# Issuing a decoder kernel's weight loads from ScalarE's DMA queue, with new costs in its planner

## The chip, the cores and the metric

The kernel runs on one core of a Trainium2 chip. The metric is the time of one execution in device microseconds, as the median of three runs. Only this core works; there is no exchange with others.

## The reference, cut to what matters

One step of a four-layer decoder is computed for a prompt of 512 tokens and for 8 sample sequences of 8 tokens, width 1024, all in float32. The layers differ in their token mixer: GLA (gated linear attention), GDN (gated DeltaNet), S5 (a diagonal state space), GLA again. Each layer is a set of input projections, the mixer, an output projection and a layer norm:

```python
for i in range(DEPTH):                      # DEPTH = 4
    kind = i % 3                            # 0 GLA, 1 GDN, 2 S5
    f, state = mixer[kind](x, weights, old_state)
    x = layer_norm(ALPHA_RES * x + f, ln_g[i], ln_b[i])
```

In GDN, each of 8 heads works in chunks and solves a unit lower triangular system per chunk (`u = solve(lhs, v * beta)`, `w = solve(lhs, kb * exp(gc))`), and then carries a 128 x 128 state from chunk to chunk. S5 runs a scan over 64 groups of 16 channels. The outputs are the new `x` and the final states of all mixers.

## The kernel before, in words

**The work.** Activations stand in SBUF with features on partitions and 576 token columns, in two halves of 288. Weights come as units of 128 x 1024 values (512 KB). A unit is loaded into one of `RAW = 3` raw buffers, then split into a high part (a copy to the rounded type fp32r, `CAST` in the profile) and a low part (raw minus high, `TENSOR_TENSOR fx<-sb,fx` on VectorE) in one of `RING = 4` slots, and used by products of high and low parts. These products are the dense work: `MATMUL ps<-fx 128x288` for projections into features, `128x256` and `128x512` for values and output projections. The mixers' own products read plain float32 (`ps<-sb`), and each of them stands as two records in the trace.

**The order.** No order is written out by hand. The program is a set of generator threads. Every engine operation passes through `Core.record` (line 252), which notes what it must wait for and gives it a cost from `Core.cost` (line 326), and `Core.run` (line 520) plays the engines' clocks forward and issues, on each engine, the ready operation of the lowest rank (line 551). The order in which `Core.issue` (line 360) calls the real instructions is the order in which they stand on each engine, and the engines then run their streams in that order, whatever the chip's own times are. Costs therefore decide nothing but the order, and, in `cp` (line 604), whether a copy goes to VectorE or ScalarE, and in `split_weights` (line 659) who makes the high part. Dense products have rank 10; a mixer's heads have ranks 3 to 7; evacuations of PSUM have rank 1. Dense work so stands where the planner believes that nothing more urgent is ready.

**DMA.** Every DMA of the kernel, weights, states, scratch copies through DRAM and outputs, is issued by SyncE (`self.sync`, an engine called `SP`). `load_weights` (line 640) puts out the weights' loads in the order of use, as far ahead as there are raw buffers; a load has to wait until the last reader of its buffer is done, which is VectorE's subtraction. In the planner, SyncE pays 0.45 us for an issue, and one transfer after another takes its bytes over 360 bytes per ns.

**GDN's steps.** `gdn_pair` (line 1430) handles two heads at a time, four pairs in all. A pair's scores begin with `128x128` transposes and products and two `64x128` products; VectorE then solves in 31 steps on rows that come back through DRAM (`scr`), and after the solve `gdn_head` (line 1648) begins with products `128x96`, `96x96` and `64x64` and goes on with a chain of `128x128` products over four chunks. Pairs are counted 0 to 3 below. `gdn_items` (line 1268) gives the dense work of the layer.

**S5's steps.** `s5_u` writes projected values to DRAM (`Ud`), and `s5_pair` (line 2160) reads them back in another layout by 8 DMAs of 72 KB, multiplies (`128x72`), and returns results through DRAM (`Yd`). The gate's weights are `s5_z` (`in_s_z` in the trace).

Of the kernel before, what the change touches and what calls it, by code (L numbers as in the profile page):

```python
# [142 lines left out]
FIXED = KT * 4 * HW + KT * P + RING * 2048 + 512 + 2 * HW + 512  # L143
WORDS = 52992 - FIXED
BLOCK = object()
ENGINES = ('PE', 'DVE', 'ACT', 'POOL', 'SP')
ACT_SETS = {
    AF.Exp: ('exp_and_others', 'natural_log_exp_and_others'), AF.Ln: ('natural_log_exp_and_others',),
# [14 lines left out]


class Op:
    __slots__ = ('eng', 'call', 'cost', 'rank', 'seq', 'pend', 'ready', 'end', 'succ', 'issued', 'tail', 'table')


class Engine:
# [14 lines left out]
class Core:  # L184
# [5 lines left out]
    def __init__(self, ctx, tc):  # L190
        nc = self.real = tc.nc
        self.fixed = ctx.enter_context(tc.tile_pool(name="fx", bufs=1)).tile([P, FIXED], F32R, name="fx")
        self.sb = ctx.enter_context(tc.tile_pool(name="sb", bufs=1)).tile([P, WORDS], F32, name="sb")
        self.ps = ctx.enter_context(tc.tile_pool(name="ps", bufs=1, space=PSUM)).tile([P, 4096], F32, name="ps")
        self.dram_pool = ctx.enter_context(tc.tile_pool(name="dram", bufs=1, space=DRAM))
        self.sb_name, self.ps_name = self.sb.tensor.name, self.ps.tensor.name
        self.vector, self.scalar = Engine(self, 'DVE', nc.vector), Engine(self, 'ACT', nc.scalar)
        self.gpsimd, self.tensor = Engine(self, 'POOL', nc.gpsimd), Engine(self, 'PE', nc.tensor)
        self.sync = Engine(self, 'SP', nc.sync)
        self.clock = dict.fromkeys(ENGINES, 0.0)  # L200
        self.dma = 0.0
        self.pending = dict.fromkeys(ENGINES, 0.0)
        self.queue = {e: ([], []) for e in ENGINES}
        self.ops, self.now, self.table = [], 0.0, None
        self.dense_backlog = 0

        self.region = {}
        for name, n, g in ((self.sb_name, WORDS, 16), (self.fixed.tensor.name, FIXED, 16), (self.ps_name, 4096, 32)):
            self.track(name, n, g, 4)
        self.spans, self.scratch = {}, {}  # L210
        self.bank_op = {e: np.full((4, 8), -1, np.int32) for e in ENGINES}
        self.constants = set()
        self.holes, self.used = [[0, WORDS]], {}
        self.banks = [False] * 8
        self.frees = 0
        self.threads, self.seq, self.events = [], 0, set()
        self.cur = [None, 0, 0, None, '', lambda: 0]
# [34 lines left out]
    def record(self, eng, method, fn, args, kw):  # L252
        is_ap = lambda v: isinstance(v, bass.AP)
        op = Op()
        op.eng, op.call, op.rank, op.seq = eng, (fn, args, kw), self.cur[1], len(self.ops)
        op.pend, op.ready, op.end, op.succ, op.issued, op.tail, op.table = 0, self.now, 0.0, [], False, 0.0, None
        args = list(args)
        out = kw.get('out', args[0] if args else None)
        outs, ins = [], []
        if is_ap(out):  # L260
            outs = [out] + ([kw['accum_out']] if is_ap(kw.get('accum_out')) else [])
            ins = [v for v in args[0 if 'out' in kw else 1:] if is_ap(v)]
            ins += [v for k, v in kw.items() if k not in ('out', 'accum_out') and is_ap(v)]
        self.cost(op, method, args, kw, outs, ins)
        preds, order, chain = set(), set(), set()
        for v in ins:
            s = self.span(v)
            if s is not None and (v.tensor.name, v.offset) not in self.constants:
                _, _, w, r = self.region[v.tensor.name]
                preds.update(np.unique(w[s]).tolist())  # L270
                chain.update(np.unique(r[eng][s]).tolist())
        for v in outs:
            s = self.span(v)
            if s is not None:
                _, _, w, r = self.region[v.tensor.name]
                order.update(np.unique(w[s]).tolist())
                for e in ENGINES:
                    order.update(np.unique(r[e][s]).tolist())
        for v in ins:
            s = self.span(v)  # L280
            if s is not None:
                self.region[v.tensor.name][3][eng][s] = op.seq
        for v in outs:
            s = self.span(v)
            if s is not None:
                _, _, w, r = self.region[v.tensor.name]
                w[s] = op.seq
                for e in ENGINES:
                    r[e][s] = -1

        for v in ins:
            preds.update(self.scratch.get(v.tensor.name, ()))
        for v in outs:
            if v.tensor.name in self.scratch:
                w = self.scratch[v.tensor.name]
                chain.update(w[-1:])
                w.append(op.seq)

        for v in ins + outs:
            if v.tensor.name == self.ps_name:  # L300
                rows, _ = self.span(v)
                c0 = v.offset % 4096
                s = rows, slice(c0 // 512, (c0 + sum(st * (num - 1) for st, num in list(v.ap)[1:])) // 512 + 1)
                for e in ENGINES:
                    (chain if e == eng else order).update(np.unique(self.bank_op[e][s]).tolist())
                self.bank_op[eng][s] = op.seq
        order -= preds
        chain -= preds | order
        for ids, kind in ((preds, 0), (order, 1), (chain, 2)):
            for i in ids - {-1}:  # L310
                q = self.ops[i]
                lat = None if kind == 2 else latency(q.eng, eng) if not kind or q.eng != eng else 0.0
                if q.issued:
                    if lat is not None:
                        op.ready = max(op.ready, q.end + lat)
                else:
                    op.pend += 1
                    q.succ.append((op, lat))
        self.ops.append(op)
        self.pending[eng] += op.cost  # L320
        if eng == 'PE' and op.rank >= 10:
            self.dense_backlog += 1
        if not op.pend:
            heappush(self.queue[eng][0], (op.ready, op.seq, op))

    def cost(self, op, method, args, kw, outs, ins):

        eng = op.eng
        column = any(v.shape[-1] == 1 for v in ins) or len(outs) > 1
        if not outs:  # L330
            op.cost, op.table = 1.28, args[0]
            return
        out = outs[0]
        size = lambda v: prod(v.shape[1:])
        n = size(out) if eng == 'PE' else max(size(v) for v in outs + ins)
        if eng == 'PE':
            m = 0.107 * size(ins[0]) / P if method != 'transpose' else 0.0
            if method == 'transpose':
                op.cost = n * 0.85e-3
            elif kw['lhsT'].dtype == F32R:  # L340
                op.cost = max(n * 0.417e-3, m)
            else:
                op.cost = 2 * max(n * 0.833e-3, m)
        elif eng == 'DVE':
            in_ps = any(v.tensor.name == self.ps_name for v in outs + ins)
            op.cost = 0.07 + n / 960.0 * (0.5 if not in_ps and method in ('tensor_copy', 'tensor_scalar') else 1)
            if column:
                op.cost += 0.06
        elif eng == 'ACT':
            sb = all(v.tensor.name != self.ps_name for v in ins)  # L350
            op.cost = 0.05 + 0.835e-3 * n + (0.043 if sb else 0.0) + (0.093 if column else 0.0)
            op.table = ACT_SETS.get(args[2] if len(args) > 2 else None)
        elif eng == 'POOL':
            op.cost = 0.3 + 0.165 * n if kw.get('op') == ALU.pow else 0.12 + 2.2e-3 * n
            if method == 'memset':
                op.cost = 0.1 + 0.6e-3 * n
        else:
            op.cost, op.tail = 0.45, prod(out.shape) * 4 / 360e3

    def issue(self, op):  # L360
        e = op.eng
        t = max(self.now, op.ready)
        if op.table is not None:
            sets = op.table if isinstance(op.table, tuple) else (op.table,)
            if self.table not in sets:
# [2 lines left out]
                    t += 1.28  # L368
        self.clock[e] = t + op.cost
        op.end = t + op.cost  # L370
        if e == 'SP':
            self.dma = max(self.dma, op.end + 0.7) + op.tail
            op.end = self.dma + 1.0
        op.issued = True
# [194 lines left out]
class Kernel(Core):  # L569
# [70 lines left out]
    def load_weights(self, limit):  # L640
        while limit and self.loaded < min(len(self.flat), self.split + RAW):
            src, raw = self.flat[self.loaded][0].rearrange("p a b -> p (a b)"), self.raw[self.loaded % RAW]
            for cs in self.pieces(self.loaded):
                self.sync.dma_start(out=raw[:, cs], in_=src[:, cs])
            self.loaded += 1
            limit -= 1

# [1675 lines left out]
```

## Time and profile before

| what | value |
|---|---|
| median of three runs (lowest, highest) | 1359.83 us (1357.68, 1359.98) |
| the profiled execution | 1360.72 us |
| its span in the trace | 1358.9 us |
| TensorE, VectorE, ScalarE, GpSimd busy | 94%, 70%, 44%, 12% |
| mean granted clock of TensorE | 0.96 |
| moved by DMA | 198.35 MB, 146 GB/s mean |

The profiled execution is 0.9 us above the median, and 1.8 us of it lie outside the span. Granted clock is the share of full speed that TensorE was given; in this profile it moves between two levels, 1.0 and 0.5, so that a mean of 0.75 over a stretch says that half of the stretch was at half speed. PE is TensorE's matmul, PEld its weight load, DVE is VectorE, ACT ScalarE, POOL GpSimd, and SPq SyncE's queue of DMA issues. All instructions have line 379, the planner's call, so that groups are told apart by their operands: `fx` holds activations and split weights, `sb` everything else in SBUF, `ps` is PSUM.

### The profile page before, as it was taken

To read this page: it belongs to the slowest core of one execution; us is meant where nothing else is said; L and a number is where in the kernel's file an instruction comes from. 1 tells how busy PE (TensorE), PEld (TensorE's weight loads), DVE (VectorE), ACT (ScalarE), POOL (GpSimd) and SP (SyncE) were. 2 spreads that over 40 slices of the span, in tenths; PEclk is the share of its full clock that TensorE was granted. 3 is DMA by queue.
4 is the path that set the end of the run, shared out by engine and by line. 5 is a ranking of instruction groups with operands and counts; after the bars stand their busy time and mean duration, and the time that the engine had idled before them with its cause. 6 is when DMAs were issued, how large, how long until landed. Compare 5 with 4: busy or idle time off the path is not lost.

```text
span 1358.9 us, 23510 instructions
## 1 busy us (share of the span) xinstructions
PE 1274.3 (94%) x8795; PEld 1193.2 (88%) x8795; DVE 953.4 (70%) x2087; ACT 601.9 (44%) x1341; POOL 163.0 (12%) x303
## 2 busy tenths in 40 slices
PE   8999998989996798899999889999999999999997
PEld 8999997869895698799988788999998899999985
DVE  5888888798999788778678519355334867665557
ACT  5554355224855665534542224346123245443430
POOL 5510000021211121112101000000000200000001
PEclk8999999989996899899999888899999999999999
DMA  6335546334456826274374598773325332332342
GB/s 233 106 106 167 183 149 209 128 103 141 126 147 192 235 65 189 54 177 131 118 246 128 186 238 211 202 197 86 109 78 178 104 122 98 129 129 98 124 147 70
DMA packets 129538, 198.35 MB, mean 146 GB/s; under 512 B 47176, under 2 KB 85961, under 8 KB 127377
## 3 DMA queue, kind: packets, MB, share of 16 engines
q1 hardware_dynamic: 129424, 196.86, 48.0%
q8 instruction: 69, 1.13, 0.4%
q14 instruction: 45, 0.36, 0.1%
HBM read 153.64 MB, written 47.37 MB: 148 GB/s over the span
## 4 chain that ended last, share of the span: by engine, by line
PE 76%; DVE 12%; DMA 5%; ACT 3%; issue 2%; SPq 2%; POOLq 0%; POOL 0%; DVEq 0%; ACTq 0%
PE ps L379 76%; DVE sb L379 9%; DVE fx L379 3%; ACT sb L379 2%; SPq L379 2%; DMA sb<-scr 1%; DMA sb<-Ud 1%; DMA sb<-in_s_z 1%; ACT fx L379 1%; DMA out_conv<-sb 0%; DMA sb<-in_gla_s 0%; DMA Ud<-sb 0%; DMA sb<-in_xT 0%; DMA Yd<-sb 0%; DMA sb<-in_gdn_s 0%
## 5 line engine op out<-in xcount | busy, mean ns | idle before, releaser
L379 PE MATMUL ps<-fx 128*128 128x288 f32 (+2 forms) x6736 | 1048.6, 313 | 21.1 <-DVE fx L379 7.9
L379 PEld LDWEIGHTS ps<-fx 128*128 128x128 f32 x6736 | 957.0, 192 | 70.8 <-DVE fx L379 10.4
L379 ACT CAST fx<-sb 128x1024 fp32r<-128x1024 f32 (+5 forms) x318 | 227.2, 743 | 315.9 <-PE ps L379 277.0
L379 DVE TENSOR_TENSOR fx<-sb,fx 128x1024 fp32r<-128x1024 f32 (+5 forms) x308 | 253.2, 846 | 158.1 <-ACT fx L379 143.3
L379 PE MATMUL ps<-sb 128*128 128x128 f32 (+10 forms) x2059 | 302.5, 299 | 54.1 <-DVE sb L379 20.2
L379 PEld LDWEIGHTS ps<-sb 128*128 128x128 f32 (+6 forms) x2059 | 252.7, 180 | 85.2 <-ACT sb L379 24.2
L379 DVE TENSOR_TENSOR sb<-sb 128x128 f32<-128x128 f32 (+32 forms) x667 | 262.0, 416 | 20.6 <-ACT sb L379 6.5
L379 ACT COPY sb<-ps 128x512 f32<-128x512 f32 (+10 forms) x247 | 94.4, 404 | 158.8 <-PE ps L379 96.8
L379 DVE SCALAR_TENSOR_TENSOR sb<-sb 128x600 f32<-128x600 f32 (+7 forms) x205 | 133.8, 661 | 13.2 <-ACT sb L379 6.9
L379 ACT ACTIVATE sb<-sb 128x128 f32<-128x128 f32 (+10 forms) x241 | 108.0, 501 | 65.8 <-DVE sb L379 57.5
L379 DVE SCALAR_TENSOR_TENSOR sb<-sb,ps 128x256 f32<-128x256 f32 (+3 forms) x216 | 92.9, 458 | 61.3 <-PE ps L379 44.7
L379 POOL TENSOR_TENSOR sb<-sb 128x1 f32<-128x1 f32 (+4 forms) x46 | 75.8, 1653 | 468.4 <-DVE sb L379 446.1
L379 ACT ACTIVATE sb<-ps 128x128 f32<-128x128 f32 (+2 forms) x176 | 67.0, 385 | 73.7 <-PE ps L379 42.9
L379 DVE SCALAR_TENSOR_TENSOR sb<-ps,sb 128x128 f32<-128x128 f32 (+3 forms) x112 | 55.7, 505 | 44.3 <-PE ps L379 40.7
L379 DVE COPY sb<-ps 128x256 f32<-128x256 f32 (+6 forms) x85 | 34.2, 407 | 66.0 <-PE ps L379 36.7
L379 POOL COPY sb<-sb 128x24 f32<-128x24 f32 (+4 forms) x92 | 35.9, 413 | 280.0 <-DVE sb L379 161.5
L379 POOL MEMSET sb<- 128x8 f32 (+9 forms) x96 | 28.5, 315 | 203.7 <-DVE sb L379 143.7
L379 ACT ACTIVATE sb<-ps,sb 128x128 f32<-128x128 f32 (+2 forms) x98 | 40.7, 435 | 22.6 <-PE ps L379 21.8
L379 ACT CAST fx<-ps 128x512 fp32r<-128x512 f32 (+2 forms) x32 | 17.6, 550 | 72.5 <-PE ps L379 69.5
L379 ACT ACT_TABLE_LOAD x31 | 39.8, 1283 | 1.7 <-PEq L2312 0.7
L379 POOL CAST fx<-sb 128x32 fp32r<-128x32 f32 (+1 forms) x33 | 10.8, 357 | 217.8 <-PE ps L379 217.8
L379 ACT ACTIVATION_READ_ACCUMULATOR sb<-ps 128x1 f32 x136 | 27.8, 204 | 0.0
(25 smaller groups left out, 245.9 us busy)
## 6 DMA issues: line engine op xcount, KB each, us to landing
sb<-in_gla_v SPq DMA_DIRECT2D x16, 512.0 KB, 4.1
sb<-in_gla_r SPq DMA_DIRECT2D x16, 512.0 KB, 3.6
sb<-in_gla_s SPq DMA_DIRECT2D x8, 1024.0 KB, 5.7
out_s_gla<-sb SPq DMA_DIRECT2D x8, 1024.0 KB, 5.1
sb<-in_gla_out SPq DMA_DIRECT2D x16, 512.0 KB, 4.1
sb<-in_gdn_s SPq DMA_DIRECT2D x32, 256.0 KB, 3.2
sb<-in_s_glu SPq DMA_DIRECT2D x16, 512.0 KB, 3.7
xres<-sb SPq DMA_DIRECT2D x12, 512.0 KB, 4.5
```

The costliest lines, as they stand in the source:

```text
L379: fn(*args, **kw)
```

## The change

Two things change. `load_weights` issues the load of every weight unit after the first three from ScalarE instead of SyncE. The order's planner gets an attribute `by` beside `eng`: `eng` is the engine whose instruction stream holds the operation, `by` is what carries it out, and for a DMA `by` stays SyncE's transfer model. And the planner's costs are new: TensorE's products a few per cent dearer, a doubled cost for a product that is planned behind a time in which TensorE was planned idle (`granted`), a DMA's transfer by the length of its contiguous runs, 0.1 us for an issue on ScalarE.

```diff
+        op.by = 'SP' if method == 'dma_start' else eng
...
-                lat = None if kind == 2 else latency(q.eng, eng) if not kind or q.eng != eng else 0.0
+                lat = None if kind == 2 else latency(q.by, eng) if not kind or q.by != op.by else 0.0
...
-            m = 0.107 * size(ins[0]) / P if method != 'transpose' else 0.0
+            m = 0.111 * size(ins[0]) / P
             if method == 'transpose':
-                op.cost = n * 0.85e-3
+                op.cost = max(n * 0.867e-3, 0.06)
             elif kw['lhsT'].dtype == F32R:
-                op.cost = max(n * 0.417e-3, m)
+                op.cost = max(8e-3 + n * 0.434e-3, m)
             else:
-                op.cost = 2 * max(n * 0.833e-3, m)
+                op.cost = 2 * max(n * 0.843e-3, m, 0.055)
...
-            op.cost, op.tail = 0.45, prod(out.shape) * 4 / 360e3
+            run = min(self.run_of(v) for v in outs + ins)
+            op.cost, op.tail = 0.45 if op.eng == 'SP' else 0.1, prod(out.shape) / run * (8e-3 + 0.188e-3 * run) / 16
...
     def issue(self, op):
         e = op.eng
         t = max(self.now, op.ready)
+        if e == 'PE' and not self.granted(t):
+            op.cost *= 2
+            self.pending[e] += op.cost / 2
...
-        if e == 'SP':
+        if op.by == 'SP':
             self.dma = max(self.dma, op.end + 0.7) + op.tail
             op.end = self.dma + 1.0
...
             for cs in self.pieces(self.loaded):
-                self.sync.dma_start(out=raw[:, cs], in_=src[:, cs])
+                (self.scalar if self.loaded > 2 else self.sync).dma_start(out=raw[:, cs], in_=src[:, cs])
```

`run_of` counts the contiguous values in the innermost dimensions of an operand.

In the built program 144 DMA issues leave SyncE's stream and stand in ScalarE's; the 8 of the first three units stay. The counts of TensorE's and GpSimd's instructions stay. VectorE has 53 instructions more and ScalarE, its DMA issues and three more table loads aside, 53 fewer, nearly all of them copies out of PSUM or scalings of 128 x 128. And the order changes on every engine. Three places of it follow.

On TensorE, in GDN's first half, the scores of pair 1 (`x10`, `64x128 x2`) and what follows up to the first products of pair 0's heads (`128x96`), before the change:

```order
L379 MATMUL ps<-sb 128x128 x10
L379 MATMUL ps<-sb 64x128 x2
L379 MATMUL ps<-sb 128x128 x4
L379 MATMUL ps<-fx 128x288 x12
L379 MATMUL ps<-sb 128x256 x2
L379 MATMUL ps<-fx 128x288 x14
L379 MATMUL ps<-sb 128x128 x4
L379 MATMUL ps<-fx 128x288 x20
L379 MATMUL ps<-sb 128x256 x2
L379 MATMUL ps<-fx 128x288 x2
L379 MATMUL ps<-sb 128x256 x4
L379 MATMUL ps<-fx 128x288 x67
```

And with the change, the same place in two pieces, its start and its end:

```order
L408 MATMUL ps<-sb 128x128 x10
L408 MATMUL ps<-sb 64x128 x2
L408 MATMUL ps<-fx 128x288 x88
L408 MATMUL ps<-sb 128x128 x4
L408 MATMUL ps<-fx 128x288 x21
```

```order
L408 MATMUL ps<-sb 128x256 x2
L408 MATMUL ps<-fx 128x288 x20
L408 MATMUL ps<-sb 128x256 x2
L408 MATMUL ps<-fx 128x288 x224
L408 MATMUL ps<-sb 128x96 x8
```

Before, no dense product stood between the first two groups of pair 1's scores, and 115 up to pair 0's heads; now it is 88 and 420.

On TensorE, at the end of GDN, the heads of the last pair (`128x96` to `64x64`), before the change:

```order
L379 MATMUL ps<-sb 96x96 x6
L379 MATMUL ps<-fx 128x288 x4
L379 MATMUL ps<-sb 128x128
L379 MATMUL ps<-fx 128x288
L379 MATMUL ps<-sb 128x128
L379 MATMUL ps<-sb 96x96 x4
L379 MATMUL ps<-sb 128x128
L379 MATMUL ps<-sb 64x64 x4
L379 MATMUL ps<-sb 128x128 x14
L379 MATMUL ps<-sb 64x64 x4
L379 MATMUL ps<-fx 128x288 x6
```

And with the change, the end of pair 2's heads and the whole start of pair 3's:

```order
L408 MATMUL ps<-sb 64x64 x4
L408 MATMUL ps<-sb 128x128 x11
L408 MATMUL ps<-sb 128x96 x8
L408 MATMUL ps<-sb 128x128 x2
L408 MATMUL ps<-sb 96x96 x4
L408 MATMUL ps<-fx 128x512
L408 MATMUL ps<-sb 128x128
L408 MATMUL ps<-sb 96x96 x8
L408 MATMUL ps<-sb 128x128 x4
L408 MATMUL ps<-sb 96x96 x4
L408 MATMUL ps<-sb 128x128 x5
```

Before, pairs 2 and 3 stood some 435 products apart, with dense work among them; now pair 3's heads begin 48 products behind pair 2's, the projections' dense work is used up ahead of them, and from the first product of pair 2's heads on, 151 products hold one dense one.

On SyncE, where S5 begins, the copies through DRAM (`Ud`) and the gate's weights (`in_s_z`), before the change:

```order
L379 DMA sb<-in_s_z 128x1024 x2
L379 DMA sb<-Ud_71 16x16x72 x4
L379 DMA sb<-s5G 128x1024
L379 DMA Ud_72<-sb 128x576
L379 DMA sb<-s5R 128x1536
L379 DMA sb<-Ud_71 16x16x72 x4
L379 DMA sb<-in_s_z 128x1024
L379 DMA sb<-Ud_72 16x16x72 x4
```

And ScalarE's stream with the change, around its loads of the same weights:

```order
L408 CAST fx<-sb 128x1024
L408 DMA sb<-in_s_u 128x1024
L408 DMA sb<-in_s_z 128x1024 x2
L408 COPY sb<-ps 128x64x8
L408 CAST fx<-sb 128x1024
L408 DMA sb<-in_s_z 128x1024
L408 CAST fx<-sb 128x1024
```

Before, the third load of the gate stood behind eight reads of `Ud`; now the loads stand between ScalarE's casts and its copies out of PSUM, and SyncE's stream has the `Ud` copies without them. The last `128x72` product of S5 has 87 more instructions ahead of it on TensorE than before, dense ones.

## Rows read from the trace of the kernel before

**Rows 1.** The page's span, and busy shares by engine

```profile
span 1358.9 us, 23510 instructions
...
PE 1274.3 (94%) x8795; PEld 1193.2 (88%) x8795; DVE 953.4 (70%) x2087; ACT 601.9 (44%) x1341; POOL 163.0 (12%) x303
```

**Rows 2.** Busy time by stretch: length, PE, PEld, DVE, ACT, POOL (instructions), granted clock, DMA

```profile
225.00:325.00 100.00, 87.52 (x486) 73.37 (x486) 84.39 (x163) 33.32 (x62) 12.03 (x23) 0.95 0.49 159
...
404.60:446.80 42.20, 27.93 (x153) 25.43 (x154) 38.49 (x144) 23.74 (x71) 7.99 (x26) 0.76 0.70 201
446.80:485.80 39.00, 30.48 (x205) 27.66 (x203) 28.80 (x84) 21.04 (x60) 3.17 (x7) 0.78 0.68 177
485.80:566.00 80.20, 70.01 (x491) 64.99 (x491) 71.79 (x224) 50.29 (x166) 13.27 (x34) 0.94 0.44 120
566.00:740.00 174.00, 173.02 (x1220) 159.61 (x1219) 128.08 (x317) 76.12 (x214) 28.94 (x48) 1.00 0.50 146
...
775.00:871.00 96.00, 85.33 (x598) 84.37 (x596) 51.26 (x74) 33.21 (x70) 1.18 (x6) 0.88 0.86 217
...
1100.00:1343.90 243.90, 243.90 (x1687) 229.45 (x1686) 149.51 (x291) 102.60 (x211) 12.23 (x27) 1.00 0.34 113
```

**Rows 3.** The page's chain of waits that ended last, by engine

```profile
PE 76%; DVE 12%; DMA 5%; ACT 3%; issue 2%; SPq 2%; POOLq 0%; POOL 0%; DVEq 0%; ACTq 0%
```

**Rows 4.** TensorE in order of time, 380 to 435 us: start, length, instruction

```profile
380.21 24.21 PE L379 MATMUL ps<-fx 128*128 128x288 f32 x179
404.69 1.68 PE L379 MATMUL ps<-sb 128*128 128x128 f32 x14 [0.27 <-ACT sb L379]
414.72 1.12 PE L379 MATMUL ps<-sb 128*128 128x128 f32 x4 [8.35 <-ACT sb L379]
416.43 3.25 PE L379 MATMUL ps<-fx 128*128 128x288 f32 x12 [0.59 <-DVE fx L379]
...
432.21 2.07 PE L379 MATMUL ps<-sb 128*128 128x256 f32 x4 [4.25 <-DVE sb L379]
```

**Rows 5.** TensorE in order of time, one run of 128x128 products, full clock

```profile
647.67 6.68 PE L379 MATMUL ps<-sb 128*128 128x128 f32 x60
```

**Rows 6.** Loads of two weights on SyncE's queue: issue ns, who waited, landing

```profile
L379 SPq DMA_DIRECT2D sb<-in_gla_out x16: 327/328/333, 174.0 to 1306.9; - x16
...
L379 SPq DMA_DIRECT2D sb<-in_s_z x8: 333/408/447, 781.6 to 858.6; - x8
...
  PE ps L379: 5.4, 1
...
DMA to landing us min/median/max: 3.6/5.9/9.9
```

**Rows 7.** The chain in order of time, 785 to 803 us

```profile
785.35 9.24 DMA sb<-Ud
794.60 8.34 DMA sb<-in_s_z
```

**Rows 8.** SyncE in order of time: first and last weight load of two stretches

```profile
416.44 0.35 SPq L379 DMA_DIRECT2D sb<-in_gdn_q  x1
...
551.22 0.35 SPq L379 DMA_DIRECT2D sb<-in_gdn_v  x1
...
778.89 0.33 SPq L379 DMA_DIRECT2D sb<-in_s_u  x1
...
858.60 0.42 SPq L379 DMA_DIRECT2D sb<-in_s_z  x1
```

**Rows 9.** Who waited for whom: us in total, times, longest

```profile
ACT fx L379 <- PE ps L379: 346.4, 124, 9.8
...
ACT sb L379 <- DVE sb L379: 153.5, 93, 8.4
...
SPq L379 <- DVE fx L379: 461.1, 105, 14.9
```

**Rows 10.** The page's groups: VectorE's copies out of PSUM

```profile
L379 DVE COPY sb<-ps 128x256 f32<-128x256 f32 (+6 forms) x85 | 34.2, 407 | 66.0 <-PE ps L379 36.7
```

More of the change, by code (lines that the diff above doesn't have):

```diff
@@ L145 @@
 BLOCK = object()
+WINDOW = 3.413
 ENGINES = ('PE', 'DVE', 'ACT', 'POOL', 'SP')
@@ L165 @@
 class Op:
-    __slots__ = ('eng', 'call', 'cost', 'rank', 'seq', 'pend', 'ready', 'end', 'succ', 'issued', 'tail', 'table')
+    __slots__ = ('eng', 'by', 'call', 'cost', 'rank', 'seq', 'pend', 'ready', 'end', 'succ', 'issued', 'tail', 'table')
 class Engine:
@@ L205, in __init__ @@
         self.dense_backlog = 0
+        self.idle = {}
         self.region = {}
@@ L326, in cost @@
     def cost(self, op, method, args, kw, outs, ins):
-        eng = op.eng
+        eng = op.by
         column = any(v.shape[-1] == 1 for v in ins) or len(outs) > 1
@@ L357, in cost, with run_of, granted @@
         else:
-            op.cost, op.tail = 0.45, prod(out.shape) * 4 / 360e3
+            run = min(self.run_of(v) for v in outs + ins)
+            op.cost, op.tail = 0.45 if op.eng == 'SP' else 0.1, prod(out.shape) / run * (8e-3 + 0.188e-3 * run) / 16
+    def run_of(self, ap):
+        dims = list(ap.ap)
+        if ap.tensor.name in self.region:
+            dims = dims[1:]
+        n = 1
+        for step, num in reversed(dims):
+            if num > 1 and step != n:
+                break
+            n *= num
+        return n
+    def granted(self, t):
+        a = max(self.clock['PE'], t - 4 * WINDOW)
+        while a < t - 1e-6:
+            w = int(a / WINDOW + 1e-9)
+            e = min(t, (w + 1) * WINDOW)
+            self.idle[w] = self.idle.get(w, 0.0) + e - a
+            a = e
+        return self.idle.get(int(t / WINDOW) - 1, 0.0) < 0.4 * WINDOW
     def issue(self, op):
```

## The prediction

> **What bounds the kernel now.** The page's shares come first: TensorE is busy 1274.3 of 1358.9 us, the next engine 953.4 [rows 1]. The chain of waits says the same: three quarters of it are TensorE's, and all DMA is 5%, SyncE's issues 2% [rows 3]. What a new order can win is thus what TensorE loses, and the table by stretch shows where that is. I read two losses from each row: idle time (length less busy) and, as an estimate, one minus the granted clock, times busy time, for products that ran at 1.2 instead of 2.4 GHz. The long GLA stretch from 1100 us on loses nothing, and GDN's last third (566 to 740) loses 1 us. The losses are at GDN's start: 14.3 idle and 6.7 by the clock, 21.0 us, from 404.6 to 446.8; 8.5 and 6.7, 15.2 us, to 485.8; 10.2 and 4.2, 14.4 us, to 566; then 10.7 and 10.2, 20.9 us, in S5 from 775 to 871; and 16.9 us around the first layer norm, from 225 to 325 [rows 2]. The clock fell after idle time in each case and cannot be won apart from it. These five make 88 us, and no forecast may claim more than a part of that.
>
> TensorE in order of time shows what the first of them is. 179 dense products of 288 columns run without a gap in 24.21 us, 0.135 us each; then come pair 1's scores, and TensorE, in order, stands 8.35 us for the next group of them, released by ScalarE, and later 4.25 us for VectorE [rows 4]. The old plan cost such a product at 0.417 ns a column, 0.120 us; the new one at 0.133. The old plan also took cheap transfers for the scratch copies on which VectorE's solves wait. It believed TensorE ahead of where it really is, and the mixers' steps earlier than they are.
>
> **Part by part.**
>
> *The first GDN stretch.* Ahead of pair 0's heads stand 305 dense products more than before, 305 x 0.135 = 41 us of work that is ready [rows 4]; 88 of them, 11.9 us, lie exactly where 8.35 us were lost. Cover of 41 us for a loss of 21.0 is enough by size, but one engine still has its late moments: I take 17 won. Ends: 21 won, or nothing, if the late step (VectorE is busy 38.49 of these 42.20 us [rows 2]) moves back by as much.
>
> *What that cover is missing from.* Dense work is not made, only moved. The heads of pairs 2 and 3 now run one behind the other, 151 products of which one is dense. A 128 x 128 product takes two records of 0.111 us [rows 5], so 150 mixer products are at most 33 us of work, and chains between engines wait in it. The nearest row of such a bare stretch is the one from 446.8 to 485.8, which lost 15.2 us with one pair [rows 2]. Here four heads instead of two can fill each other's gaps, and this end of GDN had lost nothing. I take 8 lost; ends 0 and 25 (that row's 15.2 and the 10.2 idle of the row behind it once more).
>
> *S5.* The chain goes through eight reads of `Ud` and then 8.34 us through one load of the gate's weights that stood behind them in SyncE's stream [rows 7]; TensorE waited 5.4 us for it, and such loads landed after 3.6 to 9.9 us [rows 6]. With the change they stand early in ScalarE's stream, so this wait goes. What is late next is `Ud` itself (9.24 us in the chain), whose reads are not moved. There are also 87 more dense products ahead of the last of S5's products (12 us of cover). I take 8 of 20.9 won; ends 0 and 20.9. The Trainium skill speaks against more here: "DMA: Bandwidth & Descriptors", section "Issuing engines are not separate DMA queues", says that DMAs of all issuing engines share the same 16 engines and interleave, and that a second issuer saves no more than issue time. By that, a load next to `Ud` lands no sooner for its queue, and the term would be about the 5.4 us of earlier issue. The rows neither show nor exclude it, as all the traffic has one queue.
>
> *ScalarE pays for the issues.* No row shows an issue on ScalarE. On SyncE it takes 327 to 447 ns [rows 6]. 144 of them are 47 to 64 us in a stream that is busy for 601.9 [rows 1], almost all beside a busy TensorE. In the losing stretches of GDN and S5 SyncE now issues 13 and 9 weight loads [rows 8], and I count 22 for ScalarE there: 7 to 10 us, of which ScalarE's 3% of the chain sees little. I take 2 lost; ends 0 and 10.
>
> *ScalarE waits for the raw buffer.* SyncE waited 461.1 us in all, 105 times, for VectorE's last reading of buffers, with nothing urgent behind it in most cases [rows 9]. On ScalarE, evacuations of PSUM and the heads' scalings queue behind such a load, and TensorE waits for those. The plan puts a load where it believes VectorE done, so that only the error of the plan is waited for; the nearest row is ScalarE's waits for VectorE, 153.5 us in 93 waits, 1.65 us each [rows 9]. 22 x 1.65 = 36 us is the upper end, 0 the lower; I take 2, as ScalarE now also waits 346.4 us for TensorE to free slots before its weight casts, a sign of the old TensorE cost, and a better cost leaves room.
>
> *VectorE's 53 further instructions* at 0.407 us [rows 10] are 22 us, of which what falls between 404 and 566 counts, where it is nearly full. I take 2 lost, ends 0 and 8. The other places (the layer norm's 16.9, the 14.4 up to 566) are reordered without a reason that I can read; a plan with truer costs should win some: 6 won, ends 15 won and 8 lost.
>
> Sum: -17 + 8 - 8 + 2 + 2 + 2 - 6 = -17 us. The profiled execution took 1360.7, which gives 1343.7; it stands 0.9 above the median, so 1342.8, rounded 1343 us, 1.2% less. A measurement of this kernel can tell about 0.2%, 2.7 us, from no change.
>
> **The rivals.**
>
> *ScalarE's stream becomes the wait (slower).* One load too early by a few us holds all evacuations behind it. Against: SyncE's long waits are those of an idle queue. For: in GDN and S5 a step of the chain on ScalarE often follows VectorE closely. Its price is the 36 us above; with 1.65 us on each of 22 loads passed on in full, and the rest of the sum as it is (-17 - 2 of waits counted), the result is +17, 1377 us. It decides from about 0.9 us per load on, where 19 us eat the gain.
>
> *The gain is given back at the end of GDN.* If the bare stretch of pairs 2 and 3 costs 25 and not 8, the sum is 0, and the time 1360. For: the layer's dense work is the same and was fully used there before.
>
> *More is won.* If the truer costs close two thirds of the 71.5 us lost in GDN's three stretches and in S5, as an order made for these durations might, and the losses above stay at 14, it is -34, 1326 us. For: each gap read in the rows got its cover in the new order. Against: VectorE at 70 to 90% in GDN sets the solves' pace, and no order changes that.
>
> *The queue itself gives nothing* (the rule above): S5 gains 5 and not 8, 1346 us; inside the forecast, so that its chance, about one in two, moves nothing.
>
> That the change does not do what it says is out: 144 issues do stand in ScalarE's stream.
>
> **How the numbers follow.** Forecast (1328 to 1356): 0.50. More won (below 1328): 0.18. Given back, within 0.2%: 0.08. Slower by more: 0.24, of which ScalarE's wait has 0.15 and a bare end of GDN together with small mishaps 0.09. So faster 0.68, same 0.08, slower 0.24. The range goes from 1318, part of the way into the case of more, to 1368, halfway to the rival of ScalarE's wait.
>
> **What would show it.** Right: in GDN's first half TensorE has no gap of several us between pair 1's scores, and the clock stays up until pair 0's heads; the `in_s_z` loads land without TensorE waiting; issues on ScalarE take some 0.3 to 0.45 us. Step two is wrong if TensorE is idle over 10 us in the last 60 us before GDN's output projection. ScalarE's rival is right if waits of ScalarE's issues for VectorE's splits sum to over 50 us and evacuations with them come late. The forecast as a whole is wrong if GDN from its first scores to its output projection is not at least 8 us shorter.

## The result, and the profile after

The changed kernel took **1392.3 us** (median; 1389.0 to 1396.6) beside 1359.9 us for the kernel before on the same chip: ratio 1.025, 95% interval 1.022 to 1.028. The forecast was 1343 us, 1318 to 1368: wrong in its side and its range. Three of the runs below stood far off and are in no ratio: one of e5 (2467 us), one of e15 (1573 us) and one of the kernel before beside e13 to e15 (3255 us). The page after, span and shares, against [rows 1], then its DMA queues (packets, MB, share):

```profile
span 1388.4 us, 23464 instructions
...
PE 1281.6 (92%) x8795; PEld 1196.3 (86%) x8795; DVE 970.9 (70%) x2140; ACT 590.2 (43%) x1291; POOL 163.0 (12%) x303
...
q1 hardware_dynamic: 108688, 121.35, 28.8%
q10 hardware_dynamic: 20736, 75.51, 17.4%
```

TensorE does the same 8795 products in a span 29.5 us longer; the second queue carries the moved 75.51 MB. The stretches of the changed kernel, with the columns of [rows 2]: most of GDN (four rows), then S5 from its first to its last `128x72` product.

```profile
400.00:480.00 80.00, 78.89 (x583) 77.67 (x583) 71.86 (x171) 49.05 (x115) 21.05 (x55) 1.00 0.65 172
480.00:600.00 120.00, 106.88 (x809) 98.75 (x807) 91.89 (x297) 75.84 (x228) 17.54 (x35) 0.99 0.43 124
600.00:663.40 63.40, 44.62 (x310) 42.94 (x311) 52.21 (x164) 25.24 (x56) 10.74 (x24) 0.87 0.52 144
663.40:752.30 88.90, 86.10 (x523) 73.29 (x522) 66.50 (x161) 33.94 (x107) 10.80 (x15) 1.00 0.42 138
801.20:956.50 155.30, 132.89 (x880) 130.92 (x881) 72.72 (x107) 50.09 (x91) 1.57 (x7) 0.81 0.59 158
```

The same S5 stretch of the kernel before:

```profile
803.09:918.30 115.21, 109.93 (x806) 109.17 (x807) 62.53 (x90) 44.82 (x84) 1.51 (x7) 0.90 0.77 208
```

GDN's start is full at the whole clock, as forecast. S5 begins 2 us earlier than before and ends 38 us later, with 74 products more in it (some 10 us at 0.135). Its loss, counted as in the prediction (idle time plus one minus granted clock, times busy), went from 5.3 + 11.0 = 16.3 us to 22.4 + 25.2 = 47.7 us. All else together came out about even.

S5's middle shows how. SyncE in order of time (start, length, queue, DMA, count):

```profile
858.63 20.66 SPq L408 DMA_DIRECT2D Yd<-sb  x8
879.38 0.40 SPq L408 DMA_DIRECT2D sb<-s5Kx  x1
...
892.36 21.41 SPq L408 DMA_DIRECT2D Yd<-sb  x13
...
915.98 0.54 SPq L408 DMA_DIRECT2D sb<-s5G  x1
```

TensorE there, and what it stood idle for:

```profile
867.23 8.77 PE L408 MATMUL ps<-fx 128*128 128x288 f32 x51
883.75 0.67 PE L408 MATMUL ps<-sb 128*128 128x72 f32 x2 [7.75 <-DMA sb<-s5Kx]
...
901.63 11.73 PE L408 MATMUL ps<-fx 128*128 128x288 f32 x74
920.66 3.69 PE L408 MATMUL ps<-sb 128*128 128x72 f32 x16 [7.30 <-DMA sb<-s5G]
```

ScalarE, which now issues the weights (ACTq):

```profile
872.71 1.05 ACT L408 CAST fx<-sb 128x1024 fp32r<-128x1024 f32 x1 [4.53 <-PE ps L408]
873.77 1.28 ACT L408 ACT_TABLE_LOAD   x1
875.05 0.33 ACTq L408 DMA_DIRECT2D sb<-in_s_glu  x1
...
906.60 1.05 ACT L408 CAST fx<-sb 128x1024 fp32r<-128x1024 f32 x1 [2.18 <-PE ps L408]
907.67 1.28 ACT L408 ACT_TABLE_LOAD   x1
908.94 0.33 ACTq L408 DMA_DIRECT2D sb<-in_s_glu  x1
```

And SyncE's waits from 855 to 925 us (total, times, longest):

```profile
SPq L408 <- DMA sb<-in_s_glu: 27.0, 2, 14.5
SPq L408 <- ACT sb L408: 10.3, 2, 7.4
```

Eight small stores of `Yd` take 20.66 us, since SyncE waits for loads of `in_s_glu`, with which `Yd` shares no data. The program's listing of SyncE's stream, with the semaphores that each DMA waits on, tells why (the first four of the eight):

```
DMA Yd_75<-sb 16x16x72 [waits DMAHW5_49,Activation_49]
DMA Yd_75<-sb 16x16x72 [waits DMAHW6_49]
DMA Yd_75<-sb 16x16x72 [waits DMAHW7_49]
DMA Yd_75<-sb 16x16x72 [waits DMAHW0_49]
```

The framework gives each DMA of SyncE or ScalarE one of eight completion semaphores, in turn, in the order in which the program issues them; a DMA waits until the one before it on its semaphore has landed. With one queue that is nearly always long past: in the kernel before, SyncE's waits for weight loads sum to 16 us. With two, a DMA of SyncE can wait for a load that ScalarE, in order, has not reached. In the listing the second store's wait on DMAHW6 is for a load of `in_s_glu` by ScalarE, the seventh store's wait on DMAHW3 is for the next such load, and 102 waits in SyncE's stream are for loads of ScalarE's. Here one late load leads to the next. ScalarE's load stands behind a weight cast, the cast waits for TensorE to free a slot, TensorE had waited for `s5Kx`, and that stood behind the `Yd` stores that waited for the load before. At 875.05 ScalarE issues the load; loads of `in_s_glu` land 3.7 us later in the median; at 879.4 SyncE goes on. At 908.94 the same again. I call this the **coupling**.

### The profile page after: what moved, and what is told of

Read it like the earlier page. It is cut to its first block, busy times and chain, and to the rows that moved or that the text cites. A ratio compares the mean times of both kernels' runs of the same rounds, so it can differ in the third digit from the quotient of the medians.

```text
span 1388.4 us, 23464 instructions
## 1 busy us (share of the span) xinstructions
PE 1281.6 (92%) x8795; PEld 1196.3 (86%) x8795; DVE 970.9 (70%) x2140; ACT 590.2 (43%) x1291; POOL 163.0 (12%) x303
## 3 DMA queue, kind: packets, MB, share of 16 engines
q10 hardware_dynamic: 20736, 75.51, 17.4%
## 5 line engine op out<-in xcount | busy, mean ns | idle before, releaser
L408 ACT CAST fx<-sb 128x1024 fp32r<-128x1024 f32 (+5 forms) x315 | 220.6, 732 | 334.4 <-PE ps L408 295.3
L408 PEld LDWEIGHTS ps<-sb 128*128 128x128 f32 (+7 forms) x2059 | 251.1, 180 | 98.1 <-issue 32.5
L408 DVE TENSOR_TENSOR sb<-sb 128x64 f32<-128x64 f32 (+25 forms) x667 | 263.8, 416 | 20.5 <-ACT sb L408 5.6
L408 ACT ACTIVATE sb<-sb 128x128 f32<-128x128 f32 (+7 forms) x228 | 105.4, 506 | 91.1 <-DVE sb L408 84.6
L408 ACT COPY sb<-ps 128x512 f32<-128x512 f32 (+11 forms) x224 | 88.9, 416 | 127.8 <-PE ps L408 63.5
L408 DVE COPY sb<-ps 128x256 f32<-128x256 f32 (+8 forms) x108 | 41.2, 385 | 84.0 <-ACT sb L408 62.4
L408 POOL COPY sb<-sb 128x24 f32<-128x24 f32 (+4 forms) x92 | 42.5, 485 | 325.9 <-DVE sb L408 204.8
L408 POOL MEMSET sb<- 128x3 f32 (+9 forms) x96 | 28.2, 310 | 169.7 <-PE ps L408 74.5
L408 ACT ACTIVATE sb<-ps,sb 128x128 f32<-128x128 f32 (+2 forms) x79 | 33.9, 445 | 21.5 <-PE ps L408 19.4
L408 DVE TENSOR_SCALAR sb<-ps,sb 128x128 f32<-128x128 f32 (+2 forms) x55 | 22.8, 423 | 12.3 <-ACT sb L408 11.5
```

What stands on the lines that cost most here:

```text
L408: fn(*args, **kw)
```

## The experiments

Theory A: the coupling. Theory B: the corrected estimate (the planner's new durations) makes a worse order. Theory C: any new order scatters the time. D (the order of the dense products before S5), E (the transfers themselves collide) and F (ScalarE's own stream is late) are tested further down. Each ratio is against the kernel before, run beside it. Loads are those of the weights.

**1 and 2. Each half of the change alone.**

```
# e1: after, loads back on SyncE
-(self.scalar if self.loaded > 2 else self.sync).dma_start(...)
+self.sync.dma_start(...)
# e2: after, old durations, old DMA tail, no granted()
-op.cost = max(8e-3 + n * 0.434e-3, m)
+op.cost = max(n * 0.417e-3, m)
...
```

> All weight loads back on SyncE, the corrected estimate kept. In the changed kernel S5 takes some 28 us longer than its work, and SyncE's DMAs there wait for weight loads of ScalarE's stream (27 us for in_s_glu between 855 and 925 us). Theory A (the two queues are coupled: SyncE's DMAs wait on the completion of loads that ScalarE, in order, has not issued yet): SyncE has no waits for weight loads left, S5's TensorE gaps behind s5Kx and s5G go, and the time falls by about the 28 us of S5, to 1355-1370 us. Theory B (the corrected estimate makes a worse order by itself): it stays at 1385-1395 us with the loss still in S5. Theory C (any new plan scatters the time by a per cent or two, and neither part has a cause of its own): anywhere from 1345 to 1390 us, with losses in other places than either kernel's.

> Loads on ScalarE's queue as in the changed kernel, TensorE's and the transfers' estimates as before and no model of the clock. Theory A (coupled queues): SyncE waits for weight loads again, by 50 us or more in all, and the time is 1375-1400 us. Theory B (the corrected estimate is at fault): 1350-1365 us. Theory C (scatter of plans): between 1345 and 1390 us, and the time does not follow SyncE's waits for weight loads.

Measured: costs alone 1345.4 us, ratio 0.989 (0.986 to 0.992), S5's loss 16.0 us; queue alone 1393.1 us, 1.025 (1.019 to 1.031), S5's loss 43.1 us. The rows of SyncE's waits for weight loads sum to 148 us in the second, 19 in the first, 176 in the changed kernel, 16 before. B falls: the corrected estimate gains, by more than A had expected (1355 to 1370 us). The queue costs 33 us under the old estimate and 47 under the corrected one.

**3 and 4. S5's loads on the other queue, first try.**

> The changed kernel with S5's own weight loads (in_s_u, in_s_z, in_s_glu, in_s_out) back on SyncE, all others on ScalarE. Theory A (coupled queues): S5's copies through DRAM no longer meet a load that ScalarE has not issued; the window from the first to the last 128x72 product falls from 155 us to 125-135 us, and the time to 1362-1372 us. Theory B (the corrected estimate): S5 stays at 150 us or more, 1385-1395 us. Theory D (ScalarE itself pays for issues and waits in S5, without SyncE's part): S5 falls too, but then SyncE's waits for weight loads in the changed kernel were beside the point, and TensorE's gaps behind s5Kx and s5G stay.

> The converse: only S5's weight loads are issued by ScalarE, all others by SyncE, the corrected estimate kept. Theory A (coupled queues): S5 keeps its loss (window from the first to the last 128x72 product 145-160 us) with SyncE waiting for in_s_glu, and GDN's second half loses less than in the changed kernel: 1375-1390 us. Theory B (the corrected estimate): 1385-1395 us. If both this and the run with S5's loads on SyncE lie below 1370 us, it is not the queue of S5's loads but the draw of the plan (theory C).

Measured: 1392.8 and 1346.9 us. The condition on the weight's name (`in_s_`) matched none, so these are the changed kernel and the costs alone once more. They test nothing, but show that both times repeat within 2 us. The losses of single traces repeat less well: S5's is 41.4 us in e3's trace, against 47.7 of the same program, and 15.4 in e4's, against 16.0.

**5 and 6. S5's 40 loads on SyncE, or they alone on ScalarE.**

```
# e5
+(self.scalar if self.loaded > 2 and 's5_' not in src.tensor.name else self.sync).dma_start(...)
# e6
+(self.scalar if 's5_' in src.tensor.name else self.sync).dma_start(...)
```

> The filter of the earlier pair of runs matched no weight (the arrays of S5 have names that begin otherwise), so those two repeated the changed kernel and the costs alone. Here S5's 40 loads truly stand on SyncE, all others on ScalarE; TensorE's order is the changed kernel's but for 19 lines of difference that begin in S5. Loss below is idle time plus (1 - granted clock) x busy time; in S5, from the first to the last 128x72 product, it is 47.7 us in the changed kernel, 16.3 before, 16.0 with the costs alone. Theory A (in S5 SyncE's copies wait on semaphores of loads that ScalarE, in order, has not issued yet): S5's loss falls to 15-22 us and the time to 1360-1370 us. Theory D (S5's loss comes from the order of the dense products, which the plan with ScalarE's loads made worse before S5): S5's loss stays above 40 us, 1388-1395 us.

> The converse of the run with S5's loads on SyncE: S5's 40 loads on ScalarE, all others on SyncE; up to S5 the order is that of the costs alone (1345 us). Theory A (coupling in S5): S5's loss rises from 16 to 40-48 us with SyncE waiting for in_s_glu by 20 us or more, time 1370-1380 us. Theory D (order before S5): 1343-1350 us as the costs alone.

Measured: 1365.4 us, 1.004 (1.001 to 1.007), and 1368.2 us, 1.008 (1.005 to 1.010). S5 of e5, with the 880 products of the changed kernel's S5:

```profile
803.85:927.80 123.95, 116.15 (x880) 114.11 (x881) 73.43 (x107) 50.08 (x91) 1.57 (x7) 0.96 0.74 201
```

And SyncE's same stores in it:

```profile
856.54 7.16 SPq L408 DMA_DIRECT2D Yd<-sb  x8
863.80 0.40 SPq L408 DMA_DIRECT2D sb<-s5Kx  x1
...
878.30 8.30 SPq L408 DMA_DIRECT2D Yd<-sb  x13
```

7.16 and 8.30 us for the stores in place of 20.66 and 21.41; the stretch takes 124.0 us in place of 155.3, and its loss is 12.4 us in place of 47.7. The other way round, S5 of the costs alone, then of e6, 838 products each:

```profile
792.51:913.50 120.99, 112.86 (x838) 111.50 (x839) 66.12 (x98) 41.65 (x78) 1.36 (x7) 0.93 0.73 200
```

```profile
793.27:930.70 137.43, 117.70 (x838) 116.94 (x839) 66.48 (x97) 41.53 (x78) 1.38 (x7) 0.85 0.65 174
```

The loss rises from 16.0 to 37.4 us, with a TensorE gap of 14.7 us for `s5Kx` and 35.0 us of SyncE's waits for `in_s_glu`. Between the two kernels of each pair TensorE's order differs in at most 12 of its 8010 products (by form), so D falls. S5's loads on ScalarE cost 23 us (e6 against e1; its time and loss lie a little under what was expected of A) to 27 us (the changed kernel against e5).

**7 and 8. Without the shared semaphores.** In the listing GpSimd's DMAs have semaphores of their own, DMASW0 to 7.

```
# e7: the loads issued by GpSimd
+(self.gpsimd if self.loaded > 2 else self.sync).dma_start(...)
# e8: loads on ScalarE; in s5_pair the stores and reads of Yd, and s5G, s5Kx, s5C
-self.load(st, None, src)
+self.gpsimd.dma_start(out=st, in_=src)
...
```

> All weight loads but the first three issued by GpSimd: off SyncE's stream as in the change, but neither in ScalarE's stream nor among the eight completion semaphores that SyncE's DMAs use. Theory A (coupling through the semaphores): no wait of SyncE for weight loads, S5's loss 15-22 us, time 1340-1360 us. Theory E (loads outside SyncE's stream run into S5's copies whoever issues them, by sharing the transfer engines): S5's loss stays over 35 us and the time over 1375 us. The order is planned anew, so some 10 us either way come from that.

> The changed kernel with all weight loads on ScalarE, but S5's stores and reads of Yd and its loads of s5G, s5Kx and s5C issued by GpSimd, on other completion semaphores than the weight loads. The Ud copies stay on SyncE. ScalarE's stream and TensorE's order stay the changed kernel's up to S5. Theory A (coupling through the semaphores): TensorE's long waits for s5Kx and s5G (7.7 and 7.3 us) go, S5's loss falls below 30 us, time 1365-1378 us. Theory F (no semaphores: the loads stand too late in ScalarE's own stream, and TensorE waits for the weights' casts): S5's loss stays above 40 us, with TensorE's gaps now released by ScalarE, 1385-1395 us. GpSimd may take longer per issue than SyncE; if it shows 1 us or more each, part of the gain is eaten by that.

Measured: e7 1352.7 us, 0.996 (0.993 to 0.999), S5's loss 12.6 us, and SyncE waited 1.9 us in all for weight loads. S5's loss is below what was expected, and the time 7 us above the costs alone, in another order. So loads outside SyncE's stream do not cost 47 us as such, and E falls. e8 1378.3 us, 1.015 (1.011 to 1.020), at the upper edge of what A expected: its waits for `s5Kx` and `s5G` went from 9.9 and 9.7 us to

```profile
PE ps L408 <- DMA sb<-s5Kx: 3.3, 3, 2.5
...
PE ps L408 <- DMA sb<-s5G: 2.4, 1, 2.4
```

with ScalarE's loads left where they were, and S5's loss from 47.7 to 23.9 us; 14 us of the time come back, of the 27 that e5 gets back. F falls as the main cause. The 11.5 us that remain over e5's 12.4 are what ScalarE's stream itself, the `Ud` copies left on SyncE (6.8 us of waits for weights) and 62 GpSimd issues at 541 to 731 ns (means by group) may cost; not told apart.

**9 to 12. GLA's loads alone, and how far an order scatters.**

```
# e9
+(self.scalar if self.loaded > 2 and 'gla' in src.tensor.name else self.sync).dma_start(...)
# e10 (on before), e11 (on e1)
-op.cost = 0.07 + n / 960.0 * ...
+op.cost = 0.072 + n / 960.0 * ...
# e12 (on e1)
-if e == 'PE' and not self.granted(t):
-    op.cost *= 2
-    self.pending[e] += op.cost / 2
```

> Only the weights of the two GLA layers (the first three loads apart) are issued by ScalarE; GDN's and S5's stand on SyncE, corrected estimate kept. The order is planned anew and differs from the costs alone (1345 us) from the first layer on. Theory A (coupling, which costs where SyncE has copies through DRAM that somebody waits for): the loss in S5 stays at 12-17 us, and since GLA's copies are few and not urgent, the time is 1340-1355 us, against 1365 us when GDN's loads stand on ScalarE as well. If it is 1360 us or more, what the run with S5's loads on SyncE left over (some 20 us against the costs alone) comes from ScalarE's stream in general and not from GDN's copies.

> The kernel before with one estimate nudged: VectorE's fixed cost of an instruction 0.072 instead of 0.070 us, which nobody could call more or less true, but which gives another order of the same work. It measures how far a new draw of the plan scatters the time by itself. Theory C (the effects seen are draws of the plan): 10 us or more away from before's 1360 us, either way. Otherwise within 5 us of it.

> The costs alone (all loads on SyncE, 1345 us) with the same nudge of VectorE's fixed cost, 0.072 for 0.070 us: a second draw of the order under the corrected estimate. If the corrected estimate is worth its 15 us, this stays at 1340-1352 us; if that gain was a lucky draw (theory C), it is 1353-1370 us.

> The costs alone without the model of the granted clock, that is with corrected durations of products and transfers only. If the gain is that of truer durations, as the prediction argued: 1340-1352 us. If the model of the clock (a product counted double after idle time) brings it: 1353-1362 us. A draw of the plan adds what the two nudged runs show.

Measured: e9 1362.8 us, 1.000 (0.998 to 1.003), S5's loss 16.6 us as expected, but the time above what A expected and past the mark of 1360 us that was set for a cost of ScalarE's stream in general; e10 1353.9 us, 0.994 (0.992 to 0.997), 8 us under the kernel before beside it and so between its two marks; e11 1341.4 us, 0.984 (0.979 to 0.989); e12 1341.9 us, 0.985 (0.981 to 0.990). Such a nudge, which only draws another order, moved the time by 0.6 and 0.5% here (e10, e11) and by 1.1 and 0.7% below (e14, e15), so C holds for effects of that size. Three orders under the corrected durations lie 1.1 to 1.6% below the kernel before, two under the old ones at it and 0.6% below: as far as five orders tell, the corrected durations gain, though the nearest two (e1 and e10) are only half a per cent apart; and the model of the clock adds nothing that shows. e11 and e12 beat both kernels.

**13 to 15. GDN's loads alone; second draws.**

```
# e13
+(self.scalar if 'gdn' in src.tensor.name else self.sync).dma_start(...)
# e14 (on e9): 0.071 for 0.07; e15 (on after): 0.069 for 0.07
```

> Only GDN's weights are issued by ScalarE, GLA's and S5's by SyncE, corrected estimate kept; the order is that of the costs alone (1345 us) up to GDN. If the coupling of the queues costs in GDN too, whose scratch copies stand on SyncE: the loss of the second layer rises from 56 us to 65 us or more, 1352-1365 us. If it costs only in S5: the second layer's loss stays at 50-60 us and the time at 1340-1352 us, as the prediction's step on GDN had it.

> GLA's loads alone on ScalarE once more, VectorE's fixed cost nudged to 0.071 for another draw of the order. If loads in ScalarE's stream cost in the GLA layers: 1357-1368 us again, with 22 us or more lost in the first layer (17-19 with the loads on SyncE). If the 1363 us was a draw: 1338-1355 us.

> The changed kernel with VectorE's fixed cost nudged to 0.069 for 0.070 us: another order, all loads on ScalarE. If the loss in S5 is the coupling, it comes back in any order: S5's layer loses 45 us or more (56.6 in the changed kernel, 18.6 with the costs alone) and the time is 1378-1400 us. If the 1392 us is a draw: below 1375 us.

Measured: e13 1367.4 us, 1.006 (1.004 to 1.009), a little above the expected range; e14 1374.8 us, 1.011 (1.005 to 1.018), its runs far apart (1365.7 to 1382.8), above both of its ranges; e15 1383.3 us, 1.018 (1.014 to 1.021), its S5 loses 38.3 us from the first to the last `128x72` product and 38.9 in the layer, less than the 45 expected, but more than the layer loses in any order with all loads on SyncE (16.5 to 31.8 us in six traces). The change is slower in another order too. In e13 the coupling is seen in GDN, on the scratch reads that VectorE's solves wait for. SyncE, and then ScalarE:

```profile
407.87 13.70 SPq L408 DMA_DIRECT2D sb<-scr  x2
```

```profile
417.63 0.34 ACTq L408 DMA_DIRECT2D sb<-in_gdn_k  x1
```

SyncE's waits in that stretch, 407 to 422 us:

```profile
SPq L408 <- DMA sb<-in_gdn_k: 13.1, 1, 13.1
```

VectorE waited 19.5 us for `scr` reads in e13, 0.4 in the costs alone.

**Loss by layer.** From the same views, in windows of 10 us; a layer ends with the last `128x512` product of its output projection. The loads on ScalarE are in bold.

| kernel | 1st GLA | GDN | S5 | 2nd GLA | span |
|---|---|---|---|---|---|
| before | 14.6 | 66.5 | 30.9 | 11.3 | 1358.9 |
| change | **26.4** | **52.4** | **56.6** | **10.8** | 1388.4 |
| e1, costs alone | 18.8 | 56.2 | 18.6 | 10.6 | 1348.1 |
| e5, S5 on SyncE | **24.4** | **56.4** | 23.7 | **10.5** | 1360.8 |
| e6, S5 alone | 17.1 | 55.8 | **40.1** | 10.7 | 1366.8 |
| e13, GDN alone | 18.0 | **69.6** | 27.3 | 10.2 | 1372.0 |
| e9, GLA alone | **22.3** | 57.7 | 22.2 | **10.7** | 1360.8 |

Orders scatter these losses, so one pair in the table can mislead. S5 is clear. From its first to its last `128x72` product, the five runs with S5's loads on ScalarE and `Yd` on SyncE (change, e2, e3, e6, e15) lose 37.4 to 47.7 us. All others but e8 lose 12.4 to 22.6.

GDN is not clear. With its loads alone on ScalarE it loses 13 us more than in the costs alone, but in the orders with its loads on SyncE it loses anything from 36.0 (e12) to 66.5 us (before). So e13 shows that the coupling occurs in GDN, not what it costs there. In the changed kernel and e5 the first pair's heads begin at 483.5 and 484.5 us, behind more dense work, against 447.9 in the costs alone; that this covers the coupled copies is not shown.

In the first GLA layer the loads on ScalarE go with 3 to 8 us more than in the costs alone, but e11, with all loads on SyncE, loses 23.0 us there too, and in e9 SyncE's waits for weights are no longer than with the costs alone (21 us of the whole run against 19). Why e9 and e14 are 1.1 to 2.2% slower than the costs alone **stays open**; draws of 0.5 to 1.1% can make up a part of it. What the queue costs beside S5 stays open too: e5 is 20 us above the costs alone.

The losses rose by 22.9 us of the span's 29.5. The other 6.6 us lie in TensorE's busy time (1274.3 to 1281.6), which the granted clock of the rows does not explain. They come with the corrected durations and not with the queue: the span less its losses is 1236 to 1240 us under the old durations (before, e2, e10) and 1242 to 1249 under the corrected ones, whoever issues the loads. Why is not known.

## Why the prediction was wrong, step by step

- **The first GDN stretch (17 won)** was right: 400 to 480 us has 1.1 us of idle time at the full clock, and no gap of several us stands between pair 1's scores.
- **The bare stretch of pairs 2 and 3 (8 lost)** was about right. It runs from the start of pair 2's heads to the first group of dense products behind pair 3's start:

```profile
646.07:681.64 35.57, 31.98 (x287) 30.75 (x285) 26.07 (x88) 19.91 (x65) 5.13 (x8) 0.95 0.31 95
```

  That is 3.6 us idle and 1.6 by the clock, 5.2 us lost. The mark that the text set for this step (over 10 us idle in the last 60 us before the output projection) was passed all the same, with 15.9 us from 603.4 to 663.4. But 12.2 of them lie in two gaps ahead of these heads, the first of which begins at 602.0:

```profile
608.56 8.29 PE L408 MATMUL ps<-fx 128*128 128x288 f32 x49 [6.60 <-DVE sb L408]
623.85 21.22 PE L408 MATMUL ps<-fx 128*128 128x288 f32 x137 [7.00 <-DVE sb L408]
```

  In the first VectorE was busy without a break. Ahead of the second VectorE had waited 3.6 us for `scr`, whose reads on SyncE (603 to 614 us) had waited for a load on ScalarE:

```profile
SPq L408 <- DMA sb<-in_gdn_out: 5.1, 1, 5.1
```

  So the coupling is seen in the changed kernel's GDN too. GDN's loss still fell by 14 us (66.5 to 52.4; by 10 in e3's trace of the same program), where the two steps gave 9.
- **S5 (8 won, ends 0 and 20.9) is the step that failed.** No wait for `in_s_z` is left in the changed kernel.

```profile
L408 ACTq DMA_DIRECT2D sb<-in_s_z x8: 334/334/348, 780.8 to 843.5; - x8
...
DMA to landing us min/median/max: 3.5/4.8/6.8
```

  But the layer lost 25.7 us more instead of 8 less, a miss of 34 us, more than the sum's own size. The 5.4 us were misread to begin with. The listing of the kernel before has the first `128x72` product wait for the reads of `Ud`, one of `s5G` and a copy of VectorE's, not for `in_s_z`; the load that [rows 6] and [rows 7] name only stands next on the semaphore of one of these reads. Nor did S5 need its loads on ScalarE to lose less: the costs alone lose 18.6 us in the layer, against 30.9 before.

  Above all, the step treated what is left on SyncE as untouched: "`Ud` itself, whose reads are not moved". The runs put in its place that a second in-order queue is tied to the first through the program's completion semaphores. The listing of both streams with their waits was there to be read before; I had looked for who waits for data and not at who waits for a semaphore.
- **The rule on queues** (the Trainium skill, "DMA: Bandwidth & Descriptors", section "Issuing engines are not separate DMA queues") bears up for a queue without coupling: with the loads on GpSimd S5's loss is 12.6 us, against 16.0 with them on SyncE under the same estimate, and the time 7 us longer. It says what a second issuer cannot save; the cost came from elsewhere.
- **ScalarE pays for the issues (2 lost)**: an issue takes 334 ns there, inside the 0.3 to 0.45 that the text named. **ScalarE waits for the raw buffer (2 lost)**: SyncE's wait for VectorE's splits fell from 461.1 us [rows 9] to

```profile
SPq L408 <- DVE fx L408: 8.1, 4, 3.9
```

  Of ScalarE's idle time the profile puts 15.3 us down to these splits, under the 50 us that the text set as the mark of that rival:

```profile
ACT fx L408 <- DVE fx L408: 6.7, 5, 2.9
...
ACT sb L408 <- DVE fx L408: 4.3, 3, 1.9
ACT L408 <- DVE fx L408: 4.3, 2, 3.1
```

  What both terms cost in S5 is not told apart; they are among what may make up the 11.5 us of e8 over e5.
- **VectorE's further instructions (2 lost)** can't be told apart from the order. **The other places (6 won)**: the first GLA layer and its norm lost 11.8 us more instead; 4 of them come with the corrected estimate alone (e1).
- **The rivals.** "ScalarE's stream becomes the wait" (1377 us, 0.15) had the side, and the condition that a load comes later than planned. Its mechanism was another: not evacuations behind a load on ScalarE, but SyncE's copies behind a load that ScalarE has not issued. That the truer durations would win 17 us or so was right for them alone: 1341 to 1345 us in three orders. That the sum of 17 us is so near is luck in part, since 8 of it were to come from the loads' move to ScalarE, which these three do not have. The change took the gain and gave the queue some 47 us, of which S5's coupling is 23 to 27.
- **The sign for the whole** (GDN at least 8 us shorter) came: from the end of the first GLA layer's output projection to the end of its own, GDN took 439 us in place of 456. The loss lay in S5 and in the first GLA layer, where the sign did not look.

## What to carry to other kernels

Before DMAs are moved to a second queue, list both streams with their semaphore waits: where DMAs of two in-order engines take completion semaphores from one pool, a late issue on one engine stops the other's stream, whatever data they carry. Move urgent or independent traffic only to a queue whose semaphores are its own, or leave it, and look at the lateness of the engine that will issue, not at its busy share. When a planner makes the order, test each half of a change alone and nudge a number that means nothing: here such a draw was worth 0.5 to 1.1%. And where the profile names a DMA that an instruction waits for, look in the listing whether it is that DMA or another on the same semaphore.

## What was not expected of the hardware

A load's issue takes a steady 334 ns on ScalarE (334 to 389 over `in_gla_out` and `in_s_z`), where SyncE's took 327 to 447 [rows 6]. On GpSimd an `in_s_glu` load took 530 to 533 ns and landed 3.8 us later in the median, against 3.7 us from ScalarE: the slower issue left no mark on the landing.

```profile
L408 POOL DMA_DIRECT2D sb<-in_s_glu x16: 530/530/533, 836.2 to 971.9; - x16
...
DMA to landing us min/median/max: 3.5/3.8/8.3
```
